# Second mixer of a two-layer decoder: another order of its projection chunks, and its output transposed in place

## The chip, the cores and the metric

One core of a Trainium2 chip runs the whole program. The metric is the device time of one execution in microseconds (us). An engine's queue runs in the order in which the framework put it; engines wait for each other by semaphores. PE is TensorE (matrix products, results in PSUM), DVE is VectorE, ACT is ScalarE, POOL is GpSimd, and SP issues most of the loads.

## What is computed

The program computes two decoder layers on 512 tokens of width 1024 in float32. Each layer is a token mixer, a residual LayerNorm, a PEER channel mixer and another LayerNorm. The change touches the mixer of the second layer (HGRN2) alone. Cut to what matters:

```python
def mixer_c(x, w_in, lower_bound, norm_g, w_out):
    h = x @ w_in                                   # 1024 -> 4096
    q, fz, i, g = jnp.split(h, C_SPLITS, axis=-1)  # 4 x 1024, 8 heads of 128
    f = lower_bound + (1.0 - lower_bound) * jax.nn.sigmoid(fz)
    o = hgrn2_chunkwise(q, 1.0 - f, i, jnp.log(f)) # decayed scores, and a state carried along the tokens
    y = head_rmsnorm(o, norm_g) * jax.nn.silu(g)
    return y @ w_out
```

The layer then takes LayerNorm of 4**0.25 times its input plus this.

## The kernel before

**Precision.** A float32 product is made of three fast ones: each operand is split into a high part (`hi`, a cast on ACT, L76) and the rest (`lo`, a subtraction on DVE, L77), and `mm3` (L92 to L94) multiplies hi by hi, hi by lo and lo by hi. Weights come in chunks of 512 output columns, four loads of 512 KB to a chunk (`stream`, L82), through 5 raw buffers and 6 pairs of split buffers.

**Projections.** The input of the mixer stands transposed in SBUF (`xT`: `xThi`, `xTlo`, features on partitions, 8 by 512 tokens). A chunk of weights is 96 matmuls of 512 columns, in 4 tiles of 24; each tile fills one of the two `pA` buffers of PSUM and is then emptied by a sink. `proj_T` gives features by tokens, `proj_N` tokens by features, one token block (`tb`, 128 tokens) to a tile. The 4096 columns are chunks 0 and 1 (queries of heads 0 to 3 and 4 to 7), 2 and 3 (forget gates of the same heads), 4 and 5 (values), 6 and 7 (output gates). In the text W2 is chunk 2, and so on.

**Heads.** `decays(h)` prepares one head; in the text d0 to d7. On DVE: the gate f (L424, L425), a scan of five products in two shared pads (L427), the query times the scan (L431), a reciprocal (L433), and the keys derived from it (L434 to L457). On PE: 32 short score matmuls into `pC` (L463, L465, L468) and, after two more DVE steps (L471, L473), four transposes (L476). `rp` and `kout` share two buffers, and `kh` and `qh` have one each, so that DVE can't get far ahead of PE's score matmuls. `recur(grp)`, in the text r0 and r1, runs the state of four heads over the four token blocks: 80 short matmuls (L491, L496, L499), with a state update on DVE between blocks (L503, L507), and a copy of the output and its sums of squares on ACT (L511, L515). `normed(hf)` makes 1/rms of these heads (ACT L523, DVE L524) and loads the norm's gains.

**Gates and output.** The sink of W6 and W7 (`sink_g`) takes a sigmoid on ACT (L529), three products on DVE (L530, L531, L534) and the last one (L535) into the output tile `oc`. Its tile `sgc` has one buffer, so that the sigmoid of the next token block waits for L535 of this one. At the end `oc` is transposed by 8 PE transposes to a token block (L149), split into a new `xT` (ACT L154, DVE L155), and `out_proj` multiplies it by two chunks of the output weights (sink L197). The new `xT` has the same memory as the old one, and so is written only when the last projection has read the old one.

**What sets the order.** The queue of each engine follows the order of the program text, except that a later instruction is put first where the framework reckons that the earlier one is not ready. So matmuls of a later chunk fill in where PE would wait for a head. The text's order is W4, W2, W0, d0, d1, W5, d2, d3, W1, r0, W3, d4, d5, W6, d6, d7, r1, W7, the transposes, `out_proj`.

Of the kernel before, what the change touches and what calls it, by code (L numbers as in the profile page):

```python
# [9 lines left out]
F32 = mybir.dt.float32  # L10
# [10 lines left out]
P = 128  # L21
T = 512
NTB = T // P
D = 1024
# [25 lines left out]
class Kern:  # L50
# [324 lines left out]
    def mixer_c(self, xT, hs):  # L375
        nc, tc, io = self.nc, self.tc, self.io
        w = io["c_w_in"]
        c3 = "p (c s) -> p c s"
        with tc.tile_pool(name="mc", bufs=1) as mc, tc.tile_pool(name="mc2", bufs=1) as mc2:
# [17 lines left out]
            nc.vector.tensor_scalar(oml, lb, -1.0, 1.0, ALU.mult, ALU.add)  # L397

            v = mc.tile([P, NTB, D], F32, name="vi", tag="vi")
            o = mc.tile([P, NTB, D], F32, name="oc", tag="oc")  # L400
            pads = []
            for nm in ("pa", "pb"):
                t = mc.tile([P, 16, 48], F32, name=nm, tag=nm)
# [4 lines left out]
            q, kin, scs, kon, dec = {}, {}, {}, {}, {}  # L408
# [4 lines left out]
                nc.scalar.copy(q[n], ps)  # L413

            def sink_f(n, ps):
                kin[n - 8] = mc2.tile([P, T], F32, name="kin", tag="kin", bufs=5)
                nc.scalar.activation(kin[n - 8], ps, AF.Sigmoid)

            def decays(h):
# [40 lines left out]
                for tb in range(NTB):  # L460
# [3 lines left out]
                    for c in (0, 2):  # L464
# [2 lines left out]
                                         q[h][:, t0 + 32 * c + 32:t0 + 32 * c + 64], start=True, stop=True)  # L467
                    nc.tensor.matmul(pc[0:64, t0 + 64:t0 + 128], kh[:, tb].rearrange("p c s -> p (c s)"),  # L468
                                     qh[:, tb].rearrange("p c s -> p (c s)"), start=True, stop=True)
                s = mc2.tile([P, NTB, P], F32, name="scs", tag="kin", bufs=5)  # L470
                nc.vector.tensor_tensor(s, pc.rearrange("p (a b) -> p a b", a=NTB),  # L471
                                        cm[:, None, :].broadcast_to([P, NTB, P]), ALU.mult)
                nc.vector.tensor_tensor(ko4, ko4, fk[:, :, :, None].broadcast_to([P, 4, 4, 32]), ALU.mult)  # L473
# [8 lines left out]
            def recur(grp):  # L482
                state = None
                for tb in range(NTB):
                    ts = slice(tb * P, (tb + 1) * P)
                    po = self.psB.tile([P, 512], F32, name="pB", tag="pB")
                    if tb < NTB - 1:
                        pk = self.psC.tile([P, 512], F32, name="pC", tag="pC")
                        for i in range(4):
                            h = 4 * grp + i  # L490
                            nc.tensor.matmul(pk[:, i * P:(i + 1) * P], kon[h][:, ts], v[:, tb, h * P:(h + 1) * P],  # L491
                                             start=True, stop=True)
                    for i in range(4):
                        h = 4 * grp + i
                        es = slice(i * P, (i + 1) * P)
                        nc.tensor.matmul(po[:, es], scs[h][:, tb, :], v[:, tb, h * P:(h + 1) * P],  # L496
                                         start=True, stop=tb == 0)
                        if tb:
                            nc.tensor.matmul(po[:, es], q[h][:, ts], state[:, i, :], start=False, stop=True)  # L499
                    if tb < NTB - 1:  # L500
                        s2 = mc2.tile([P, 4, P], F32, name="stc", tag="stc", bufs=2)
                        if state is None:
                            nc.vector.tensor_copy(s2, pk.rearrange("p (a b) -> p a b", a=4))  # L503
                        else:
                            for i in range(4):
                                h = 4 * grp + i
                                nc.vector.scalar_tensor_tensor(s2[:, i, :], state[:, i, :], dec[h][:, tb:tb + 1],  # L507
                                                               pk[:, i * P:(i + 1) * P], ALU.mult, ALU.add)
                        state = s2
                    ov = o[:, tb, grp * 512:(grp + 1) * 512]  # L510
                    nc.scalar.copy(ov, po)  # L511
                    sq = mc2.tile([P, P], F32, name="sq", tag="sq")
                    for i in range(4):
                        h = 4 * grp + i
                        nc.scalar.activation(sq, po[:, i * P:(i + 1) * P], AF.Square, accum_out=ss[:, tb, h:h + 1])  # L515
# [3 lines left out]
            def normed(hf):  # L519
                ngs[hf] = mc.tile([P, 512], F32, name="ngc", tag="ngc")  # L520
                nc.sync.dma_start(out=ngs[hf], in_=io["hgrn_norm_g"][0][None, hf * 512:(hf + 1) * 512].broadcast_to([P, 512]))
                h4 = slice(4 * hf, 4 * hf + 4)
                nc.scalar.activation(rs[:, :, h4], ss[:, :, h4], AF.Sqrt, bias=self.epst, scale=1.0 / 128)  # L523
                nc.vector.reciprocal(rs[:, :, h4], rs[:, :, h4])  # L524

            def sink_g(j, tb, ps):
                hf = j - 6
                sg = mc2.tile([P, 512], F32, name="sgc", tag="sgc")
                nc.scalar.activation(sg, ps, AF.Sigmoid)  # L529
                nc.vector.tensor_tensor(sg, sg, ps, ALU.mult)  # L530
                nc.vector.tensor_tensor(sg, sg, ngs[hf], ALU.mult)  # L531
                ov = o[:, tb, hf * 512:(hf + 1) * 512]
                o4 = ov.rearrange("p (h e) -> p h e", h=4)
                nc.vector.tensor_tensor(o4, o4, rs[:, tb, 4 * hf:4 * hf + 4, None].broadcast_to([P, 4, P]), ALU.mult)  # L534
                nc.vector.tensor_tensor(ov, ov, sg, ALU.mult)  # L535

            def sink_v(j, tb, ps):
                nc.scalar.copy(v[:, tb, (j - 4) * 512:(j - 3) * 512], ps)

            self.proj_N(w, 4, xT, sink_v, (3, 0, 1, 2))  # L540
            self.proj_T(w, 2, xT, sink_f)
            self.proj_T(w, 0, xT, sink_q)
            decays(0)
            decays(1)
            self.proj_N(w, 5, xT, sink_v)
            decays(2)
            decays(3)
            self.proj_T(w, 1, xT, sink_q)
            recur(0)
            normed(0)  # L550
            self.proj_T(w, 3, xT, sink_f)
            decays(4)
            decays(5)
            self.proj_N(w, 6, xT, sink_g)
            decays(6)
            decays(7)
            recur(1)
            normed(1)
            self.proj_N(w, 7, xT, sink_g)
            yT = self.new_xT()  # L560
            for tb in range(NTB):
                self.transpose_in(o[:, tb], yT, 0, 8, tb)
        self.out_proj(io["c_w_out"], yT, hs)

    def mixer(self, layer, xT, hs):
        if layer == 0:
# [444 lines left out]
```

## Time and profile before

| what | value |
|---|---|
| time before, median of 3 runs | 2940.26 us (2937.48 to 2942.72) |
| the profiled execution's own time | 2942.42 us |
| its span, first to last instruction | 2940.7 us |
| PE busy over the span | 98% |
| DVE busy over the span | 81% |
| mean granted clock of TensorE | 0.993 |

A profile is of one execution. Busy time of PE is of modelled ends, and neighbouring matmuls overlap in it, so durations of PE work are taken here from start to start. A granted clock of 1.00 is 2.4 GHz and one of 0.50 is 1.2 GHz. Starts are in microseconds from the first instruction. The second mixer's projections start at 1404 us and its output projection at 1651 us.

### The profile page before, as it was taken

How to read it: one execution, taken by the hardware profiler on the slowest of the kernel's cores; microseconds unless marked ns; L12 is line 12 of the kernel's file. 1: busy time of each engine (PE TensorE's matmuls, PEld its weight loads, DVE VectorE, ACT ScalarE, POOL GpSimd, SP SyncE). 2: the span in 40 equal slices, each digit the busy share in tenths (PEclk: the TensorE clock that was granted, in tenths of full speed). 3: DMA queues.
4: the chain of work that ended last, by engine and by line, in shares of the span. 5: the costliest groups of instructions: out<-in, count | busy, mean ns of one | idle time of the engine just before them, and what ended most of it. 6: DMA issues, size and time to landing. Idle time of an engine off the chain costs nothing.

```text
span 2940.7 us, 42471 instructions
## 1 busy us (share of the span) xinstructions
PE 2890.8 (98%) x15822; PEld 2571.7 (87%) x15822; DVE 2387.9 (81%) x4500; ACT 1171.2 (40%) x1730; POOL 696.8 (24%) x538
## 2 busy tenths in 40 slices
PE   8999999999999999999999899999999999999998
PEld 6788999988888888888887789999988888898897
DVE  6679999788888888875758589999788887888875
ACT  3233565433333333334432433555433333333333
POOL 0000000144444444440000000000344444444420
PEclk9999999999999999999999899999999999999999
DMA  6233369999999999984221233379999999999972
GB/s 218 80 104 104 136 202 295 324 371 334 350 336 336 360 338 335 361 330 136 91 87 54 86 108 109 132 241 301 349 349 329 362 337 342 349 342 339 360 282 71
DMA packets 282927, 740.26 MB, mean 252 GB/s; under 512 B 21600, under 2 KB 120416, under 8 KB 282720
## 3 DMA queue, kind: packets, MB, share of 16 engines
q1 hardware_dynamic: 208992, 469.08, 45.9%
q0 software_dynamic: 73728, 268.47, 24.5%
q8 instruction: 124, 2.03, 0.3%
q14 instruction: 83, 0.68, 0.1%
HBM read 667.73 MB, written 69.73 MB: 251 GB/s over the span
## 4 chain that ended last, share of the span: by engine, by line
PE 89%; DVE 9%; ACT 1%; issue 1%; DMA 1%; POOL 0%; SPq 0%; ACTq 0%; POOLq 0%; DVEq 0%
PE pC L904 18%; PE pB L904 18%; PE pA L92 15%; PE pA L93 15%; PE pA L94 15%; PE pB L755 2%; PE pB L756 2%; DVE lo L77 1%; DVE s L667 1%; DVE ix L669 1%; DVE ix L666 1%; DVE stop L665 0%; PE pC L463 0%; PE pC L149 0%; DVE stop L668 0%
## 5 line engine op out<-in xcount | busy, mean ns | idle before, releaser
L77 DVE TENSOR_TENSOR lo<-raw,hi 128x1024 fp32r<-128x1024 f32 x608 | 739.7, 1218 | 204.7 <-ACT hi L76 200.7
L92 PE MATMUL pA<-xThi,hi 128*128 128x384 f32 (+2 forms) x2496 | 863.1, 346 | 12.7 <-ACT hi L76 9.5
L76 ACT CAST hi<-raw 128x1024 fp32r<-128x1024 f32 x608 | 638.2, 1052 | 589.5 <-PE pA L93 479.8
L93 PE MATMUL pA<-xTlo,hi 128*128 128x384 f32 (+2 forms) x2496 | 859.5, 344 | 0.7 <-DVE xTlo L155 0.7
L94 PE MATMUL pA<-xThi,lo 128*128 128x384 f32 (+2 forms) x2496 | 859.0, 344 | 0.0
L804 POOL DMA_INDIRECT row<-in_u,eid x256 | 390.3, 1525 | 942.2 <-DVE av L814 628.7
L92 PEld LDWEIGHTS pA<-xThi,hi 128*128 128x128 f32 x2496 | 471.1, 189 | 35.3 <-ACT hi L76 9.9
L93 PEld LDWEIGHTS pA<-xTlo,hi 128*128 128x128 f32 x2496 | 471.0, 189 | 21.7 <-DVE xTlo L155 0.9
L94 PEld LDWEIGHTS pA<-xThi,lo 128*128 128x128 f32 x2496 | 470.5, 189 | 16.3 <-DVE lo L77 1.0
L76 ACT CAST ch<-ge 128x384 fp32r<-128x384 f32 x256 | 131.6, 515 | 623.9 <-PE pC L904 505.3
L804 POOL DMA_INDIRECT row<-in_v,eid x256 | 300.1, 1172 | 179.7 <-DVE h L823 112.4
L823 DVE SCALAR_TENSOR_TENSOR h<-row,cf,h 128x1024 f32<-128x1024 f32 x256 | 328.2, 1282 | 0.0
L814 DVE CUSTOM_DVE_ANT_0 row<-row,x 128x1024 f32<-128x1024 f32 x256 | 311.3, 1217 | 0.0
L904 PE MATMUL pC<-hi,ch 128*128 128x512 f32 x768 | 300.8, 392 | 0.0
L904 PE MATMUL pB<-lo,ch 128*128 128x512 f32 x768 | 300.5, 391 | 0.0
L904 PE MATMUL pC<-hi,cl 128*128 128x512 f32 x768 | 300.0, 391 | 0.0
L904 PE MATMUL pB<-hi,cl 128*128 128x512 f32 x768 | 299.3, 390 | 0.0
L904 PE MATMUL pB<-hi,ch 128*128 128x512 f32 x768 | 298.9, 389 | 0.0
L904 PE MATMUL pC<-lo,ch 128*128 128x512 f32 x768 | 298.5, 389 | 0.0
L77 DVE TENSOR_TENSOR cl<-ge,ch 128x384 fp32r<-128x384 f32 x256 | 142.4, 556 | 179.8 <-ACT ch L76 176.8
L904 PEld LDWEIGHTS pC<-lo,ch 128*128 128x128 f32 x768 | 144.2, 188 | 31.9
L904 PEld LDWEIGHTS pB<-hi,cl 128*128 128x128 f32 x768 | 144.0, 188 | 31.8
(247 smaller groups left out, 3446.0 us busy)
## 6 DMA issues: line engine op xcount, KB each, us to landing
raw<-in_peer_ut SPq DMA_DIRECT2D x256, 512.0 KB
raw<-in_peer_v SPq DMA_DIRECT2D x256, 512.0 KB
gd<-gbuf SPq DMA_DIRECT2D x24, 2048.0 KB
gt<-gd SPq DMA_DIRECT2D x64, 768.0 KB
sp<-ge SPq DMA_DIRECT2D x22, 768.0 KB
ge<-sp SPq DMA_DIRECT2D x22, 768.0 KB
raw<-in_peer_w_q SPq DMA_DIRECT2D x32, 512.0 KB
raw<-in_c_w_in SPq DMA_DIRECT2D x32, 512.0 KB
```

What stands on the lines that cost most here:

```text
L76: self.nc.scalar.copy(hi, src)
L77: return self.nc.vector.tensor_tensor(lo, src, hi.bitcast(F32), ALU.subtract)
L92: nc.tensor.matmul(ps, ah, bh, start=(i == 0), stop=False)
L93: nc.tensor.matmul(ps, ah, bl, start=False, stop=False)
L94: nc.tensor.matmul(ps, al, bh, start=False, stop=(i == n - 1))
L666: nc.vector.max_index(out=ix[:, 0:8], in_max=mx[:, 0:8], in_values=sc)
L755: nc.tensor.matmul(pg[:, sl], oh[:, 0, a, :, b], og[:, 0, a, :, b], start=True, stop=False)
L756: nc.tensor.matmul(pg[:, sl], oh[:, 0, a, :, b], og[:, 1, a, :, b], start=False, stop=True)
L804: nc.gpsimd.indirect_dma_start(out=t, out_offset=None, in_=io[name], in_offset=bass.IndirectOffsetOnAxis(ap=self.eid[:, j:j + 1], axis=0))
L814: nc.vector.tensor_tensor_reduce(ur, ur, x3, 1.0, 0.0, ALU.mult, ALU.add, av[:, k:k + 1])
L823: nc.vector.scalar_tensor_tensor(acc, vr, coefs[i // GQ][:, i % GQ:i % GQ + 1], acc, ALU.mult, ALU.add)
L904: nc.tensor.matmul(acc[hf], a[:, ts], b[:, hf * 512:(hf + 1) * 512], start=first and i == 0, stop=last and i == 2)
```

## The change

The order of the text in `mixer_c` becomes W4, W2, W0, d0, W3, d1, d2, W1, d3, r0, d4, W5, d5, d6, W6, d7, r1, W7: the forget gates and queries of heads 4 to 7 come before the first recurrence, and the values of heads 4 to 7 behind it. The output is no longer one tile of 16 KB to a partition: its first half is four tiles of their own, and its second half uses the buffers of the tag `kin`, of which there are 9 in place of 5. The 8 transposes of a token block are issued within W7, one block behind its projection, and are written into `xT` itself, into the 128 columns of that block, which its own tile of W7 has read; the last block's come behind W7. The number of instructions of each kind stays the same.

```diff
-            o = mc.tile([P, NTB, D], F32, name="oc", tag="oc")
+            o = {}
...
-                kin[n - 8] = mc2.tile([P, T], F32, name="kin", tag="kin", bufs=5)
+                kin[n - 8] = mc2.tile([P, T], F32, name="kin", tag="kin", bufs=9)
...
-                s = mc2.tile([P, NTB, P], F32, name="scs", tag="kin", bufs=5)
+                s = mc2.tile([P, NTB, P], F32, name="scs", tag="kin", bufs=9)
...
-                    ov = o[:, tb, grp * 512:(grp + 1) * 512]
-                    nc.scalar.copy(ov, po)
+                    if grp == 0:
+                        o[0, tb] = mc.tile([P, 512], F32, name="oc%d" % tb, tag="oc%d" % tb)
+                    else:
+                        o[1, tb] = mc2.tile([P, 512], F32, name="od", tag="kin", bufs=9)
+                    nc.scalar.copy(o[grp, tb], po)
...
-                ov = o[:, tb, hf * 512:(hf + 1) * 512]
+                ov = o[hf, tb]
...
+            def sink_last(j, tb, ps):
+                sink_g(j, tb, ps)
+                if tb:
+                    turn(tb - 1)
+
+            def turn(tb):
+                for hf in range(2):
+                    self.transpose_in(o[hf, tb], xT, 4 * hf, 4, tb)
 
             self.proj_N(w, 4, xT, sink_v, (3, 0, 1, 2))
             self.proj_T(w, 2, xT, sink_f)
             self.proj_T(w, 0, xT, sink_q)
             decays(0)
+            self.proj_T(w, 3, xT, sink_f)
             decays(1)
-            self.proj_N(w, 5, xT, sink_v)
             decays(2)
+            self.proj_T(w, 1, xT, sink_q)
             decays(3)
-            self.proj_T(w, 1, xT, sink_q)
             recur(0)
             normed(0)
-            self.proj_T(w, 3, xT, sink_f)
             decays(4)
+            self.proj_N(w, 5, xT, sink_v)
             decays(5)
+            decays(6)
             self.proj_N(w, 6, xT, sink_g)
-            decays(6)
             decays(7)
             recur(1)
             normed(1)
-            self.proj_N(w, 7, xT, sink_g)
-            yT = self.new_xT()
-            for tb in range(NTB):
-                self.transpose_in(o[:, tb], yT, 0, 8, tb)
-        self.out_proj(io["c_w_out"], yT, hs)
+            self.proj_N(w, 7, xT, sink_last)
+            turn(NTB - 1)
+        self.out_proj(io["c_w_out"], xT, hs)
```

## Rows read from the trace of the kernel before

**Rows 1.** The page's first line, and its line of busy time (share of the span) and instructions of each engine.

```profile
span 2940.7 us, 42471 instructions
PE 2890.8 (98%) x15822; PEld 2571.7 (87%) x15822; DVE 2387.9 (81%) x4500; ACT 1171.2 (40%) x1730; POOL 696.8 (24%) x538
```

**Rows 2.** Busy time by stretch, in the second mixer: the stretch, its length, the busy time of each engine with its number of instructions, the granted TensorE clock, the share of the DMA engines and GB/s. The first row is the body of the mixer, the next three are pieces of its end, and the last is the whole end.

```profile
1420.00:1611.00 191.00, 191.00 (x1013) 155.49 (x1011) 135.48 (x239) 66.17 (x119) 1.28 (x12) 1.00 0.23 75
1611.00:1619.50 8.50, 6.47 (x31) 4.87 (x30) 8.50 (x18) 0.60 (x2) 0.00 (x0) 1.00 0.30 92
1619.50:1629.80 10.30, 9.47 (x49) 8.10 (x50) 2.71 (x5) 2.50 (x10) 0.00 (x0) 0.50 0.06 24
...
1640.00:1646.80 6.80, 4.96 (x16) 4.09 (x17) 6.03 (x10) 2.26 (x4) 0.00 (x0) 0.50 0.00 0
1611.00:1651.30 40.30, 31.32 (x167) 26.17 (x166) 23.13 (x44) 16.74 (x49) 0.00 (x0) 0.79 0.11 35
```

**Rows 3.** PE in order of time at the end of the mixer: start, duration, line, output and inputs, count, and in brackets the idle time of PE before it with what ended it. The first two rows are the first and the last matmul of W7's third tile, the next three belong to d7 and the start of r1, then come the transposes behind r1 (the gap stands before the second row of them) and the first matmul of the output projection; W7's last tile runs between these two.

```profile
1611.30 0.50 PE L92 MATMUL pA<-hi,xThi 128*128 128x512 f32 x1 [0.28 <-DVE sgc L530]
...
1616.64 0.39 PE L94 MATMUL pA<-hi,xTlo 128*128 128x512 f32 x1
1618.20 0.46 PE L463 MATMUL pC<-qs,kin 128*128 128x128 f32 x2 [1.17 <-DVE fq L446]
...
1624.93 1.12 PE L476 MATMUL pC<-c_ident,kout 128*128 128x128 f32 x4 [0.56 <-DVE kout L473]
1625.84 1.49 PE L491 MATMUL pC<-vi,kon 128*128 128x128 f32 x6
...
1635.53 0.60 PE L149 MATMUL pC<-c_ident,oc 128*128 128x128 f32 x4
1641.84 1.97 PE L149 MATMUL pC<-c_ident,oc 128*128 128x128 f32 x8 [5.71 <-DVE oc L535]
...
1651.34 0.50 PE L92 MATMUL pA<-hi,xThi 128*128 128x512 f32 x1 [0.45 <-ACT xThi L154]
```

**Rows 4.** PE in order of time, at full clock: the first matmul of r0, the first of W3 behind it, the first score matmul of d4 behind W3, the first matmul of the next chunk behind those, and the ten matmuls of r1 that stand ahead of d7 in PE's queue.

```profile
1533.64 1.06 PE L491 MATMUL pC<-vi,kon 128*128 128x128 f32 x8
...
1542.62 0.48 PE L92 MATMUL pA<-xThi,hi 128*128 128x512 f32 x1
...
1564.49 0.38 PE L463 MATMUL pC<-qs,kin 128*128 128x128 f32 x2
...
1567.83 0.50 PE L92 MATMUL pA<-hi,xThi 128*128 128x512 f32 x1
...
1594.42 1.05 PE L496 MATMUL pB<-vi,scs 128*128 128x128 f32 x8
...
1605.60 0.38 PE L496 MATMUL pB<-vi,scs 128*128 128x128 f32 x2
```

**Rows 5.** ACT in order of time behind r1: the load of the table for the square root, the square root, the load of the sigmoid's table, and the sigmoid of the second token block of W7.

```profile
1637.96 1.28 ACT L523 ACT_TABLE_LOAD   x1
1639.26 0.31 ACT L523 ACTIVATE rsc<-ssq,epst 128x16 f32<-128x16 f32 x1
1639.58 1.28 ACT L529 ACT_TABLE_LOAD   x1
1641.82 0.60 ACT L529 ACTIVATE sgc<-pA 128x512 f32<-128x512 f32 x1 [0.95 <-DVE oc L535]
```

**Rows 6.** DVE in order of time at the same place: 1/rms, the last gate product of W7's first token block, and the first and the last gate product of its second.

```profile
1639.60 0.25 DVE L524 RECIPROCAL rsc<-rsc 128x16 f32<-128x16 f32 x1 [6.09 <-ACT rsc L523]
...
1641.10 0.69 DVE L535 TENSOR_TENSOR oc<-oc,sgc 128x512 f32<-128x512 f32 x1
...
1642.90 0.68 DVE L530 TENSOR_TENSOR sgc<-sgc,pA 128x512 f32<-128x512 f32 x1
...
1644.34 0.69 DVE L535 TENSOR_TENSOR oc<-oc,sgc 128x512 f32<-128x512 f32 x1
```

**Rows 7.** Busy time by stretch, columns as in rows 2: from the end of d3's work on DVE to the start of d4's, and from there to the score matmuls of d7.

```profile
1515.90:1549.40 33.50, 33.50 (x189) 29.20 (x188) 10.34 (x18) 18.00 (x49) 0.11 (x1) 1.00 0.19 64
1549.40:1620.00 70.60, 68.30 (x362) 53.81 (x360) 63.69 (x116) 16.95 (x27) 0.43 (x4) 1.00 0.20 63
```

**Rows 8.** DVE in order of time: the first step of d4, and the first and the last of its three steps behind its score matmuls.

```profile
1549.48 0.54 DVE L424 TENSOR_SCALAR pa<-kin,oml,lb 128x512 f32<-128x512 f32 x1
...
1567.94 0.69 DVE L471 TENSOR_TENSOR scs<-pC,cmask 128x512 f32<-128x512 f32 x1 [1.78 <-PE pC L468]
...
1569.15 0.69 DVE L479 TENSOR_TENSOR qs<-qs,fq 128x512 f32<-128x512 f32 x1
```

**Rows 9.** PE in order of time at the start of the mixer, where LayerNorm's output is transposed into `xT` block by block: the transposes of block 3, the first matmul of W4 on block 3, and the transposes of block 0. Below them this stretch by busy time, columns as in rows 2.

```profile
1402.43 1.03 PE L149 MATMUL pC<-c_ident,h 128*128 128x128 f32 x8
1404.22 0.50 PE L92 MATMUL pA<-hi,xThi 128*128 128x512 f32 x1 [0.75 <-ACT xThi L154]
...
1404.79 1.03 PE L149 MATMUL pC<-c_ident,h 128*128 128x128 f32 x8
...
1402.00:1420.00 18.00, 16.31 (x86) 13.07 (x85) 16.71 (x30) 9.68 (x18) 1.62 (x6) 1.00 0.41 121
```

**Rows 10.** Busy time by stretch, columns as in rows 2, of what follows the second mixer: routing, and the expert stage to shortly before the end.

```profile
1720.00:1880.00 160.00, 158.75 (x880) 145.37 (x878) 149.43 (x753) 65.59 (x90) 0.00 (x0) 1.00 0.34 115
2000.00:2930.00 930.00, 928.30 (x4876) 829.39 (x4874) 751.36 (x948) 352.96 (x509) 345.33 (x256) 1.00 0.88 319
```

## The prediction, made before the changed kernel ran

> **What bounds the kernel now.** I read the page's busy line first: PE is busy for 98% of the span, DVE for 81% [rows 1]. So PE's queue sets the time, and a change of order can give back only what PE loses. Next I cut the second mixer into stretches. From 1420 to 1611 us PE is busy for all of 191.00 us at full clock: nothing is to be had there. The whole loss lies in the end, from 1611.0 to 1651.3 us: PE is busy for 31.32 of 40.30 us, at a mean clock of 0.79 [rows 2]. The reader should see both parts of this loss: 40.30 - 31.32 = 9.0 us of idle time, and two stretches at 1.2 GHz, with 9.47 and 4.96 us of PE work in them that would take half as long at 2.4 GHz, so (9.47 + 4.96) / 2 = 7.2 us. Together 16.2 us.
>
> As a check I count the work of this end at full clock. A tile of a projection is a quarter of W3's 1564.49 - 1542.62 = 21.87 us, 5.5 us; a head's score matmuls take 1567.83 - 1564.49 = 3.3 us; a recurrence takes 1542.62 - 1533.64 = 9.0 us, of which ten matmuls in eighty stand earlier in the queue, which leaves 7.9 us [rows 4]. Eight transposes take 1.0 us [rows 9]. The end holds W7's third and fourth tile (11.0), d7 with four transposes (3.8), r1 (7.9) and twelve transposes (1.5): 24.2 us in 40.3 us, a loss of 16.1 us. Both ways agree.
>
> Third, in order of time, what PE waits for [rows 3]. There are two places. **The last head:** three tiles of W7 have already been run as filler when PE comes to d7, and it still waits on DVE, 1.17 us at 1618.20 and 0.56 us at 1624.93; behind the first of these the clock falls. With its half-clock stretch this place costs about 2.9 us of idle time (9.0 less the 5.71 and 0.45 below) + 4.7 = 7.5 us. **Behind r1:** 5.71 us before the transposes at 1641.84. They wait for the last gate product of W7's first token block, which needs 1/rms, which needs ACT to finish r1's sums, load a table and take a root: the root runs at 1639.26 us [rows 5], 1/rms at 1639.60, and L535 ends at 1641.10 + 0.69 = 1641.79, which is 6.3 us behind 1635.53 [rows 6]. Nothing is left to fill with: W7's fourth tile needs a `pA` buffer, which L530 of the second token block frees at 1642.90 + 0.68 = 1643.58, 8.1 us behind 1635.53. With 0.45 us before the output projection and 2.5 us at half clock this place costs 8.6 us.
>
> Why is DVE late at d7? From 1515.9 to 1549.4 us it is busy for only 10.34 of 33.50 us: it has done heads 0 to 3, and d4 has no forget gates, since W3 begins at 1542.62 [rows 4, 7]. From d4's start at 1549.48 on [rows 8] it is busy for 63.69 of 70.60 us, a queue that never catches up [rows 7]. That is 23.2 us of DVE time unused in the middle, and missing at the end.
>
> **The change part by part.** *Order of the chunks.* No instruction is added or dropped, so PE's work is the same; what moves is when DVE gets its inputs. W3 comes directly behind d0 and W1 behind d2, so gates and queries of heads 4 to 7 are there before r0. d4's first steps can then run in the hole of 23.2 us. Not all of it is usable: `rp` and `kout` share two buffers and `kh`, `qh` have one each, so DVE stands at most about one head ahead of PE's score matmuls. When must d7 be ready? PE came to it at 1618.20 us with three filler tiles (16.4), ten matmuls of r1 (1.1) and about 1.5 us of waits ahead; without these PE comes to it at about 1599 us. DVE came to it at about 1619.4; with the whole hole used it is ready at 1596, with two thirds of it (15 us) at 1604, and then one filler tile of 5.5 us covers the wait. So I take the 7.5 us of the last head as recovered, and expect none or one of W7's tiles ahead of r1.
>
> *Behind r1.* If at most one tile of W7 has run, at least three (16.4 us) lie behind r1, against 6.3 us to L535 and 8.1 us to the freed buffer. The second and the third tile need no `pA` buffer that waits for 1/rms: L530 of the first token block alone frees the buffer for the third. So the 5.71 us are covered, and the clock has no reason to fall: the 8.6 us go too.
>
> *Transposes within W7, in place.* The same 32 transposes, moved ahead in PE's queue and past one tile of W7 each time: this adds a wait. The transposes of a block wait for its L535, and W7's next tile stands behind them in the queue. From a tile's end to L535's the rows show, for the second token block, 1641.82 to 1644.34 + 0.69, 3.2 us [rows 5, 6]; the change leaves a whole tile, 5.5 us, between. A margin of 2.3 us: DVE also has the splits of the output weights and the evictions in this stretch, so I bound this cost between 0 and 2 us a block, three blocks, and take 1 us in all, because transposes that are reckoned not ready let a ready tile pass, as W4 passed those of block 0 [rows 9]. What in-place saves by itself is the 0.45 us before the output projection, counted above. Its condition is that reads and writes of one `xT` are kept apart by token block. W4 began on block 3 at 1404.22 while block 0 was transposed at 1404.79 only [rows 9]: for a read behind writes to other blocks this holds; for a write behind reads no row shows it.
>
> *The rest.* SP loads the same chunks in another order; the load of the second half's gains waits, as before, for W6's last use of the first half's, and the next loads queue behind it. POOL's small fills move with their heads and nothing heavy stands behind them. ACT changes tables as often as before, 1.28 us each [rows 5]. `kin` with 9 buffers has to hold at most 4 score tiles, 4 output tiles and one head at r1: no wait, and the memory is that of the 16 KB tile. I price these at 0, between -0.5 and +1 us. r0 now has d3 and d4 directly around it, 3.8 + 9.0 + 3.8 = 16.6 us of short matmuls in a row. In the end d7 and r1 stayed at half clock for the stretch behind 1619.5 although PE was busy for 9.47 of its 10.30 us [rows 2]; but r0 and single heads at full clock did not lower it [rows 4]. Price if it falls there once: 2.5 to 4.7 us by the two stretches of rows 2; I take 0 and keep this in the range.
>
> *A rule against the transposes.* In the rows, 8 transposes with 0.75 us of waiting directly behind them left the clock at 1.00 over the 18 us around [rows 9]. The Trainium skill, "TensorE: Matmul & The Clock Gate", section "PE-mode transpose", says that the full clock does not engage for transposes, which don't count as PE activity in the same way. By that rule each block of 8 between two tiles is idle time to the clock. By rows it costs nothing; it becomes a rival below.
>
> **The sum.** 16.1 us recovered, less 1 us for the transposes' wait and 1 us for a late split at the start of the output projection (both bounded between 0 and 3): 14 us. Behind the mixer PE stays the bound (928.30 of 930.00 us, and 158.75 of 160.00 in routing, where DVE has 149.43) [rows 10], so an earlier start is an earlier end. The profiled execution took 2942.42 us, 2.2 us above the median of 2940.26; from it 2928.4, from the median 2926.3. I predict 2926 us, with 2922 to 2931 for this case by the bounds above.
>
> **Rivals.** *(B) The wait behind r1 stays.* If the framework still reckons d7 late, it puts three tiles of W7 ahead of r1 again, and transposes that wait for L535 stand before the fourth. Then only the last head's 7.5 us are won: 2933 us, 2930 to 2937. For it: in rows 3 the queue was written so. Against it: the hole in rows 7. *(C) The order on PE's queue barely changes what is late.* DVE can't use its hole because of the shared buffers, and d7 is late as before: 0 to 4 us won, 2938 us. *(D) The skill's rule.* The transposes let the clock fall once or twice: 2.5 to 4.7 us each by rows 2, off the forecast: 2931 us. *(E) Slower.* A write to `xT` waits for all earlier reads of the whole pair, and a later read for all earlier writes. Then W7's third and fourth tile and the output projection each wait for a block's transposes and their eviction: 1.0 us of transposes is work, but cast and subtraction, some 1.3 us with the 0.75 us of rows 9 as the nearest wait, are idle, about 2 us at two tiles, and at the output projection the last block's whole chain, 3.2 + 1.0 + 1.3 = 5.5 us: 9.5 us idle. At half clock over W7's four tiles another 22 us are lost. The gain of 16 less 9.5 less 0 to 22: from 6 us faster to 16 us slower; it decides from the point at which the clock stays down for more than about 13 us. Typical 2948 us. Against it stand rows 9.
>
> **Chances.** Forecast 0.62, B 0.17, C 0.09, D 0.05, E 0.07. A measurement of this kernel tells about 0.2%, 5.9 us, from no change, so "faster" means below 2934.4. Forecast and D lie below it (0.67), B with about half (0.09): 0.76. Within: the other half of B 0.08, C 0.09: 0.17. Slower: E 0.07. The range must leave out no more than 0.2: from 2922, the forecast's lower bound, to 2938, which takes in B and half of C.
>
> **What will show it.** Right: PE's waits on L535 and on d7's DVE steps under 1 us each, no granted clock of 0.5 between 1420 and 1660 us, DVE busy for more than 25 of the 33.5 us of its hole, the output projection starting near 1637 us. B: a wait of 5 us on L535 remains, with three tiles of W7 ahead of r1. C: waits before d7's score matmuls. D: 0.5 in the stretch of W7 without idle time. E: waits of W7's tiles on the eviction (L154, L155). The forecast is wrong if PE shows new waits between 1474 and 1600 us, where there are none now, for example on d1 to d3 behind W3 and W1.

## The result, and the profile after

The changed kernel takes 2923.68 us (median of 4 runs, 2922.74 to 2924.39), the kernel before 2940.23 us (median of 4, 2937.48 to 2942.72). The ratio is 0.9943 with a 95% interval of 0.9932 to 0.9954, so it is faster by 16.6 us where 14 were forecast (2926 us, range 2922 to 2938).

The page of the changed kernel: its first line, the line of busy time and the row of the clock in 40 slices. The last line, behind the dots, is the row of the clock in the kernel before; its 8, the slice of the mixer's end, is gone. PE's busy time is now 99% of the span [rows 1].

```profile
span 2922.1 us, 42467 instructions
PE 2880.0 (99%) x15822; PEld 2564.3 (88%) x15822; DVE 2388.3 (82%) x4500; ACT 1170.4 (40%) x1730; POOL 697.1 (24%) x538
PEclk9999999999999999999999999999999999999999
...
PEclk9999999999999999999999899999999999999999
```

Busy time by stretch in the second mixer, columns as in rows 2: the body, the end, and the stretch that was DVE's hole.

```profile
1420.00:1611.00 191.00, 191.00 (x1066) 157.85 (x1065) 147.75 (x265) 70.19 (x139) 1.31 (x12) 1.00 0.24 80
1611.00:1640.00 29.00, 29.00 (x151) 24.42 (x151) 19.64 (x29) 16.75 (x37) 0.14 (x1) 1.00 0.22 68
1515.90:1549.40 33.50, 33.50 (x228) 28.67 (x227) 29.71 (x61) 17.16 (x51) 0.46 (x4) 1.00 0.14 48
```

The end has no idle time and no half clock: 29.00 us of PE work in 29.00 us, at 1.00, against 31.32 in 40.30 at 0.79 [rows 2]. In the hole DVE is busy for 29.71 us instead of 10.34 [rows 7].

What PE waited for from 1400 to 1720 us: line waited at, releaser, us in total, times, longest.

```profile
PE pC L149 <- DVE xTlo L155: 1.1, 1, 1.1
PE pA L92 <- ACT xThi L154: 0.7, 1, 0.7
PE pA L93 <- DVE xTlo L155: 0.7, 1, 0.7
PE pA L92 <- ACT vi L541: 0.6, 1, 0.6
PE pC L149 <- DVE h L187: 0.4, 1, 0.4
```

Four of these belong to the LayerNorms on either side of the mixer, and the 0.6 us on `vi` to W4 at its start, a wait that the kernel before has as well. The waits of rows 3 are gone. The span became 18.6 us shorter, and the trace says where: LayerNorm's transposes ahead of the mixer start 1.2 us earlier (1402.43 to 1401.22), those behind the output projection 18.6 us earlier (1697.49 to 1678.87), and the rest of the program takes as long as before. So 17.4 us come from the mixer; the 1.2 us ahead of it arise where no code changed, and I count them as a difference between two executions.

The three starts that are not in rows 9: ahead of the mixer in the changed kernel, then behind the output projection in the kernel before and in the changed one.

```profile
1401.22 1.03 PE L149 MATMUL pC<-c_ident,h 128*128 128x128 f32 x8
...
1697.49 1.48 PE L149 MATMUL pC<-c_ident,h 128*128 128x128 f32 x12
...
1678.87 1.47 PE L149 MATMUL pC<-c_ident,h 128*128 128x128 f32 x12
```

PE in order of time: d7's first score matmul, the first matmul of W7 behind r1, the transposes of token block 0, W7's third tile, and the first matmul of the output projection.

```profile
1596.65 0.38 PE L463 MATMUL pC<-qs,kin 128*128 128x128 f32 x2
...
1612.08 0.47 PE L93 MATMUL pA<-lo,xThi 128*128 128x512 f32 x1
...
1620.81 0.60 PE L149 MATMUL pC<-c_ident,oc 128*128 128x128 f32 x4
1621.24 0.60 PE L149 MATMUL pC<-c_ident,od 128*128 128x128 f32 x4
1621.60 0.48 PE L92 MATMUL pA<-hi,xThi 128*128 128x512 f32 x1
...
1634.73 0.47 PE L92 MATMUL pA<-hi,xThi 128*128 128x512 f32 x1
```

DVE in order of time: d7's last step ahead of its score matmuls, the last gate product of token block 0 (L538 here, L535 before), and the first subtraction of that block's eviction into `xT`.

```profile
1583.93 0.28 DVE L457 TENSOR_TENSOR qh<-qs,pl 128x128 f32<-128x128 f32 x1
...
1620.25 0.69 DVE L538 TENSOR_TENSOR od<-od,sgc 128x512 f32<-128x512 f32 x1
...
1622.27 0.68 DVE L155 TENSOR_TENSOR xTlo<-pC,xThi 128x512 fp32r<-128x512 f32 x1
```

The reader should see three things. d7 is ready on DVE at 1584.2 us, 12.4 us before PE comes to it. Behind r1 PE has W7 to run, 38 matmuls from 1612.08 on, and the gate product ends at 1620.94, only 0.3 us before the transposes that read it (1621.24). And W7's third tile reads `xT` from 1621.60 on while block 0 is being written into it: a read doesn't wait for earlier writes to another block, so case E didn't come about. The other half of its condition, a write behind earlier reads of other blocks, is still not shown: the eviction of block 0 starts only when the last matmul of W7's second tile has run.

### The profile page after: what moved, and what is told of

It is laid out like the page before. It is cut to its first block, busy times and chain, and to the rows that moved or that the text cites. A ratio compares the mean times of both kernels' runs of the same rounds, so it can differ in the third digit from the quotient of the medians.

```text
span 2922.1 us, 42467 instructions
## 1 busy us (share of the span) xinstructions
PE 2880.0 (99%) x15822; PEld 2564.3 (88%) x15822; DVE 2388.3 (82%) x4500; ACT 1170.4 (40%) x1730; POOL 697.1 (24%) x538
## 4 chain that ended last, share of the span: by engine, by line
PE 87%; DVE 10%; issue 1%; ACT 1%; DMA 1%; POOL 0%; SPq 0%; ACTq 0%; POOLq 0%; DVEq 0%
PE pC L914 18%; PE pB L914 18%; PE pA L92 15%; PE pA L93 15%; PE pA L94 15%; PE pB L765 2%; DVE lo L77 1%; PE pB L766 1%; DVE s L677 1%; DVE ix L679 1%; DVE ix L676 1%; DVE stop L675 0%; DVE xp L795 0%; DVE xp L794 0%; DVE oh L758 0%
## 5 line engine op out<-in xcount | busy, mean ns | idle before, releaser
L92 PEld LDWEIGHTS pA<-xThi,hi 128*128 128x128 f32 x2496 | 470.3, 188 | 34.6 <-ACT hi L76 9.2
```

The lines of the kernel that those rows point to most:

```text
L92: nc.tensor.matmul(ps, ah, bh, start=(i == 0), stop=False)
```

## The experiments

The theory: the order of the chunks lets DVE work in its hole, so d7 is on time, so little of W7 has been used as filler when r1 ends, and the rest of W7 covers the wait for 1/rms. The first rival: it is the transposition within W7 and in place that covers it. The median of the kernel before, on the same chip, is 2938.03 us beside the first four and 2941.52 us beside the last four.

**1. The order alone.**

```diff
-            self.proj_N(w, 7, xT, sink_last)
-            turn(NTB - 1)
-        self.out_proj(io["c_w_out"], xT, hs)
+            self.proj_N(w, 7, xT, sink_g)
+            yT = self.new_xT()
+            for tb in range(NTB):
+                for hf in range(2):
+                    self.transpose_in(o[hf, tb], yT, 4 * hf, 4, tb)
+        self.out_proj(io["c_w_out"], yT, hs)
```

> The new chunk order alone: the output is transposed behind W7 into a new xT, as before the change; everything else is the changed kernel. Theory (the order lets DVE use its hole, so that d7 is ready when PE comes to it and W7 is left to fill the wait behind r1): PE's waits on d7's steps and the 5.71 us before the transposes are gone here too; only the wait for the eviction before the output projection comes back, 0.5 to 2 us. Time 2924 to 2926 us, 14 to 16 us below the kernel before. Rival (the transposes within W7 are what covers the wait behind r1): only the 7.5 us of the last head are won, a wait of 5 us on L535 and a half-clock stretch stay, 2932 to 2933 us.

Measured: 2924.22 us, 0.9949 of the kernel before (0.9935 to 0.9963). What PE waited for from 1420 to 1680 us is one line:

```profile
PE pA L92 <- ACT xThi L154: 0.2, 1, 0.2
```

The gain is there without the transposition in place, which is worth the 0.2 us of this line, less than the 0.5 to 2 us expected. The rival is out.

**2. In place alone**, with the old order of chunks (the sequence of the kernel before, with `sink_last` and `turn`).

> The old chunk order with the transposes within W7 and in place, and the changed kernel's output tiles and nine kin buffers. Theory: three tiles of W7 still run ahead of d7 and r1, so the transposes and the fourth tile meet the same wait on L535; 0 to 1 us are won, 2939 to 2940 us, with granted clocks of 0.5 near 1620 and 1640 us. Rival (in place covers the wait behind r1): 8.6 us are won, 2931 to 2932 us, and the wait on L535 is under 1 us.

Measured: 2939.25 us, 1.0004 (0.9994 to 1.0013). The waits of PE, of which these are the longest two, are those of rows 3:

```profile
PE pC L149 <- DVE od L538: 6.1, 1, 6.1
PE pC L463 <- DVE fq L446: 1.2, 1, 1.2
```

No change, as the theory has it. The nine buffers of `kin`, which this kernel has as well, bring nothing by themselves either, with the old order.

**3. More work for DVE, within the slack.**

```diff
                 nc.vector.reciprocal(rp.rearrange(c3, s=32), cp)
+                for _ in range(1 if h >= 4 else 0):
+                    nc.vector.reciprocal(rp.rearrange(c3, s=32), cp)
```

> The changed kernel with the reciprocal of d4 to d7 (3.35 us on DVE) done twice, 13.4 us more of DVE work, with the same result. Theory: in the changed kernel d7's last DVE step ends at 1584.2 us and PE comes to its score matmuls at 1596.65, a slack of 12.4 us with a tile of W7 behind it as filler; so 0 to 1.5 us slower than the changed kernel, 2923.5 to 2925.5 us. Rival (DVE is the bound of the middle of the mixer, and its slack is not real): 13 us slower, 2937 us.

Measured: 2923.18 us, 0.9947 (0.9933 to 0.9961), the same as the changed kernel. d7 is ready only at 1603.0 us here, 6.4 us after PE could have used it, and W7's matmuls filled in; 25 of them were left behind r1. It is 18.8 us later than in the changed kernel, more than the 13.4 us added, because gate products of W6 and splits of W7 now stand ahead of its last steps. PE's only wait from 1420 to 1680 us (L540 is the last gate product here):

```profile
PE pC L149 <- DVE od L540: 0.3, 1, 0.3
```

**4. More than the slack.** The same with `range(3 if h >= 4 else 0)`.

> The changed kernel with that reciprocal of d4 to d7 done four times, 40.2 us more of DVE work. Theory: d7 is late by some 40.2 - 12.4 = 28 us; W7's tiles run ahead as filler (three tiles, 16.4 us), PE waits for the remaining 11 us, and the wait behind r1 returns with its half clock (8.6 us), as in the kernel before: 15 to 25 us slower than the changed kernel, 2939 to 2949 us. Rival (filler and the wait behind r1 are not linked): the wait behind r1 stays covered, 8 to 12 us slower, 2932 to 2936 us, with no wait on L535 of more than 1 us.

Measured: 2956.03 us, 32.4 us above the changed kernel and 1.0058 (1.0044 to 1.0072) of the kernel before. The three longest waits of PE, and by busy time, columns as in rows 2, the whole stretch and the three parts of it at half clock:

```profile
PE pC L465 <- DVE kin L436: 10.0, 2, 5.1
PE pC L149 <- DVE od L540: 6.0, 1, 6.0
PE pA L92 <- DVE sgc L535: 2.4, 1, 2.4
...
1584.40:1664.00 79.60, 59.43 (x286) 48.60 (x286) 61.16 (x86) 21.70 (x57) 0.00 (x0) 0.79 0.12 40
1595.50:1609.10 13.60, 10.84 (x46) 8.14 (x47) 11.60 (x21) 2.42 (x4) 0.00 (x0) 0.50 0.12 39
1633.00:1646.70 13.70, 11.52 (x60) 9.75 (x61) 8.25 (x19) 2.84 (x11) 0.00 (x0) 0.50 0.23 77
1656.90:1663.80 6.90, 5.21 (x16) 4.33 (x17) 5.93 (x10) 2.93 (x5) 0.00 (x0) 0.51 0.00 0
```

The link that the theory asserts shows: when the heads are late, the 6 us behind r1 come back, so the rival falls. The size is off. I had counted the late heads' own waits at 11 us, and they are about that (10.0 plus shorter ones), but each of the two late heads, d6 and d7, also put the clock at 1.2 GHz for some 13.7 us, and I had priced a half clock behind r1 alone. Idle time is 79.60 - 59.43 = 20.2 us. The 27.6 us of PE work at half clock would take half as long at full clock, which makes 13.8 us more. Together they are 34.0 of the 34.6 us by which this profiled span is longer than the changed kernel's.

**5. Only W3 and W5 exchanged**, the smallest edit of the order, made to the changed kernel's code with the old sequence:

```diff
             decays(0)
             decays(1)
-            self.proj_N(w, 5, xT, sink_v)
+            self.proj_T(w, 3, xT, sink_f)
...
             normed(0)
-            self.proj_T(w, 3, xT, sink_f)
+            self.proj_N(w, 5, xT, sink_v)
             decays(4)
```

> The changed kernel with the old chunk order in which only W3 and W5 have changed places (the forget gates of heads 4 to 7 where the values of these heads stood, and these behind r0); W1 stays behind d3, and d6 behind W6. Theory (what DVE lacked in its hole was W3 alone): in the kernel before, the queries of head 4 were there at 1517.5 us, at the start of the hole, so d4 can start some 30 us earlier and d7 is ready in time: 2922 to 2926 us. Rival (the queries' early place and d6 ahead of W6 are needed too): d7 is late, three tiles of W7 run ahead of r1 and the 6 us behind r1 stay, 2930 to 2936 us.

Measured: 2923.80 us, 0.9942 (0.9928 to 0.9955). DVE's hole, columns as in rows 2:

```profile
1515.90:1549.40 33.50, 33.50 (x190) 29.28 (x189) 29.80 (x62) 16.37 (x48) 0.00 (x0) 1.00 0.19 63
```

In the changed kernel's code the exchange does all of it. The queries' early place and d6 ahead of W6 add nothing to the time that can be measured, only more matmuls of W7 left behind r1 (38 instead of 26). One condition stays untested: every run with early forget gates also has the nine buffers of `kin`. By the program text up to four score tiles and four gate tiles of that tag live at once before r0, so five buffers would probably hold W3 back; no run shows it.

**6. Only d6 ahead of W6**, with the old order of chunks.

```diff
             decays(5)
+            decays(6)
             self.proj_N(w, 6, xT, sink_g)
-            decays(6)
             decays(7)
```

> The changed kernel with the old chunk order, of which only d6 has been moved ahead of W6. Theory: DVE's work between its hole and d7 is the same sum, so d7 is as late as before, and nothing is won: 2936 to 2942 us, with the 6 us wait behind r1. Rival (d6 behind the gates of W6 is what makes d7 late): 5 to 16 us won, 2924 to 2934 us.

Measured: 2935.09 us, 0.9984 (0.9975 to 0.9993), 2 to 7 us won by the interval and 6.4 by the medians. The 11 runs spread from 2932.74 to 2940.96 us, four of them above 2939; the profiled one took 2935.09. The time lies between the two ranges, so neither expectation holds as written: more than nothing is won, and as a gain the 6.4 us is inside the rival's 5 to 16, near its lower end. The waits of PE from 1420 to 1665 us, and three stretches:

```profile
PE pC L149 <- DVE od L538: 3.7, 1, 3.7
PE pB L496 <- DVE scs L471: 0.8, 1, 0.8
...
1515.90:1549.40 33.50, 33.50 (x190) 29.18 (x189) 11.60 (x21) 17.67 (x48) 0.00 (x0) 1.00 0.19 64
...
1594.80:1598.40 3.60, 2.91 (x26) 2.09 (x26) 1.82 (x3) 0.49 (x1) 0.00 (x0) 1.00 0.38 94
1598.40:1605.30 6.90, 6.73 (x18) 5.12 (x19) 6.90 (x13) 1.18 (x2) 0.00 (x0) 0.51 0.11 33
```

DVE's hole is as empty as before (11.60 us), and some 10 of the 16 us stay lost, so the cause stands as the larger part; but DVE's remaining work is put in a better order, ten matmuls of W7 are left behind r1, and the wait there is 3.7 instead of 5.7 us. In the old order the place of d6 is a smaller cause of its own.

**7. Transposes without the lag of a tile.**

```diff
                 sink_g(j, tb, ps)
-                if tb:
-                    turn(tb - 1)
+                turn(tb)
```

> The changed kernel with each token block's transposes issued directly behind its own tile of W7 instead of one tile later. Theory: transposes that are not ready let the next tile pass in PE's queue, so nothing waits for long: 0 to 1.5 us slower than the changed kernel, 2923 to 2925.5 us. Rival (PE's queue stands at each of them for the chain of 3.2 us from a tile's end to its L535 step): three or four waits of 3 us, 9 to 13 us slower, 2933 to 2937 us.

Measured: 2923.15 us, 0.9938 (0.9925 to 0.9952); from 1420 us to the end of the mixer PE waits for nothing. Here the queue's order puts the transposes where their input is ready, although the text has them earlier: the lag that the change wrote by hand is not needed.

**8. A second gate buffer in the kernel before.**

```diff
-                sg = mc2.tile([P, 512], F32, name="sgc", tag="sgc")
+                sg = mc2.tile([P, 512], F32, name="sgc", tag="sgc", bufs=2)
```

> The kernel before with two buffers in place of one for the gate tile sgc, nothing else. Theory (the wait behind r1 is for work that runs out, and the buffers only say how much of W7 may run ahead): the fourth tile of W7 runs as filler before d7 too, the 2.9 us of waits there and their half clock go, but behind r1 nothing of W7 is left, and PE waits there 7 to 9 us instead of 5.7: 2 to 6 us won, 2932 to 2936 us. Rival (the single buffer is the cause, and the fourth tile fills the wait behind r1): 8 us or more won, 2930 us or less.

Measured: 2933.95 us, 0.9973 (0.9962 to 0.9984), 7.6 us below the kernel before of its call. Its longest wait:

```profile
PE pC L149 <- DVE oc L535: 6.2, 1, 6.2
```

The wait behind r1 stays and is even longer, as the theory says, though not the 7 to 9 us that I expected; the waits at d7 and their half clock are gone. My gain of 2 to 6 us was too low: the prediction's own price of the last head's place is 7.5 us. The buffer alone doesn't cure the end. Fifteen of the 24 matmuls of W7's fourth tile are used earlier. The nine that are left behind r1 don't shorten the wait, because ACT does two casts of the output weights and an eviction between the last sums of r1 here. The square root (1637.31 us) starts 6.4 us behind r1's last matmul instead of 3.8.

**Across the runs.** The token block's transposes of the second half's output start a fixed time behind r1's last matmul: 6.8 us in runs 2, 3, 4, 5 and 6. What PE waits is that less the matmuls of W7 that are left, with their 0.23 us each, and the four first transposes: none left, 6.05 us (runs 2 and 4); 10 left, 3.74 (run 6); 25 left, 0.34 (run 3); 26 left, 0.10 (run 5, too short to stand in its row). The rows of runs 2, 4, 6 and 3:

```profile
1640.88 1.12 PE L149 MATMUL pC<-c_ident,od 128*128 128x128 f32 x4 [6.05 <-DVE od L538]
...
1658.59 1.11 PE L149 MATMUL pC<-c_ident,od 128*128 128x128 f32 x4 [6.05 <-DVE od L540]
...
1635.92 1.09 PE L149 MATMUL pC<-c_ident,od 128*128 128x128 f32 x4 [3.74 <-DVE od L538]
...
1623.87 0.66 PE L149 MATMUL pC<-c_ident,od 128*128 128x128 f32 x4 [0.34 <-DVE od L540]
```

The 6.8 us hold for these runs alone. In run 8 it is 9.0 us. In the changed kernel, with 38 matmuls left, the gate product is ready 8.9 us behind r1, so its wait of nothing has 0.3 us to spare, not more.

## Why the prediction was right

**What bounds the kernel, and the loss of 16.1 us:** right. The end has lost all its idle time and its half clock, and the mixer is 17.4 us shorter in the profiled executions. From start to start over the whole mixer, 9.0 us of these are idle time. Another 7.6 us are the half of 15.2 us of work that ran at half clock, where the prediction counted 14.4 and 7.2. For the other 0.8 us there is no test; PE's queue changes between projection matmuls and others 62 times there before and 46 times after, which may be it. The clock is at 1.00 from 1420 to 1660 us, and the output projection starts at 1634.73 us, where I had said near 1637.

**DVE's hole:** right in its cause, and runs 5 and 6 show it alone: the exchange of W3 and W5 fills the hole and brings the whole gain, and with the hole empty most of the loss stays. Of the hole's 23.2 us DVE now uses 29.71 - 10.34 = 19.4, within the 15 to 23.2 that I allowed. The size of what follows was wrong on the safe side. I expected d7 between 1596 and 1604 us, and it is ready at 1584.2: the gates of W6's later tiles and W7's splits, which stood ahead of d7 on DVE, now come behind it. Run 3 measures what this is worth: 13.4 us of DVE work cost nothing.

**Behind r1:** right. At most one tile was to be used ahead of r1, and ten matmuls were. The cover was closer than I wrote, though: the gate product ends 8.9 us behind r1's last matmul, not 6.3, since DVE has the first token block's other products and the products with 1/rms of all four blocks to do there too, and 38 matmuls of W7 last 8.7 us. That it came out without a wait is by a margin of 0.3 us.

**The transposes' wait and the late split,** 1 us each: both measured 0. These two terms are the difference between the 14 us forecast and the 16.1 us of the loss, so the gain was forecast too low, 14 us against the measured 16.6. **In place** was priced at 0.45 us, and run 1 shows 0.24.

**The rivals.** B and C: their mechanism is real (runs 2 and 4 have the 6 us wait, run 4 the late heads), but the condition, DVE late, isn't met. D: the Trainium skill's rule on transposes ("TensorE: Matmul & The Clock Gate", section "PE-mode transpose") would have let the clock fall among the blocks of eight. Here the granted clock is 1.00 from 1611 to 1640 us with all but the last transposes between projection tiles, so by this trace such bursts cost nothing in that place. E: the third tile of W7 ran while block 0 was written, so the waits of W7's tiles by which E was priced did not come. The fall of the clock in the 16 us of d3, r0 and d4 that I kept in the range did not happen either: 1.00 in the row of the hole above, which contains them.

## What to carry to other kernels

Where the bound engine stalls at the end of a stage, look for the helper engine's hole earlier in the stage: 23 us of DVE idle time at 1516 us were paid for by PE at 1618 us, and exchanging two chunks of work repaid them. Filler that the queue uses up at one late input is missing at the next wait, so two waits in a row are one problem. A second buffer that allows more filler (run 8) took away the first wait and left the second, of 6.2 us. Count what is left to run when the fixed chain starts: here 6.8 us of chain against 0.23 us a matmul told the wait in runs 2 to 6. Look at the other engines in the chain too: in run 8 work of ACT made it longer.

## What the runs showed of the hardware

The clock fell at a single short wait. In run 6 PE ran score matmuls of 128, 64 and 32 columns and then waited for 0.8 us, up to 1598.5 us; the clock fell at 1598.4, and the next 6.73 us of work ran at 0.51. Around LayerNorm's transposes 1.69 us of waits in 18 us, with projection matmuls between, left it at 1.00 [rows 9].
